# Weight tiles displaced inside their slots, so that moving and next stationary tile keep one distance, in a four-mixer transformer kernel

## The chip, the cores and the metric

The kernel runs on one core of a Trainium2 chip. The metric is device time in microseconds (us) of one execution, the median over several runs. TensorE (PE) multiplies: a 128x128 stationary tile is loaded by an LDWEIGHTS instruction, then a moving tile of 256 columns is streamed through it by a MATMUL. VectorE (DVE), ScalarE (ACT) and GpSimd (POOL) do the elementwise work; SyncE (SP) issues the transfers.

## The reference

A sequence of 256 tokens with 1,024 channels goes through four mixers (gated linear attention, differential attention, short convolution, causal block attention with ALiBi), two SwiGLU feed-forward layers and two gated embeddings, all in float32. Nearly all of the arithmetic is `norm(h) @ W` with 1,024 to 5,632 columns of W:

```
for i in range(DEPTH):                       # DEPTH = 2
    hn = rms_norm(h, norm_mix[i])
    h = h + (gla_mixer if i == 0 else diff_attn_mixer)(hn, ...)
    h = h + swiglu(rms_norm(h, norm_ffn[i]), ffn_w_in[i], ffn_w_out[i])
    gate = jax.nn.sigmoid(rms_norm(h, ple_norm[i]) @ ple_w_gate[i])
    h = h + gate * (p[i] @ ple_w_proj[i])
h = h + short_conv_mixer(rms_norm_2(h, norm_g[0]), ...)
h = h + moba_mixer(rms_norm_2(h, norm_g[1]), ...)
```

## The kernel before, in words

The activations stay on the chip. The weights, 159 MB, pass once through it in pieces of 128x1024 float32 (512 KB): a transfer into a `raw` buffer (`load`, L149 to L154), a rounded copy `whi` by ScalarE (`high`, L160) and the remainder `wlo = raw - whi` by VectorE (`low`, L169). The activations of a stage are split the same way into `xh` and `xl` (L292, L296), or `ah`, `al` inside a feed-forward layer. A product is then three float32r matmuls, high by high, high by low and low by high, in `mm3`:

```
nc.tensor.matmul(ps, lh, rh, start=first, stop=False, **kw)      # L214
nc.tensor.matmul(ps, lh, rl, start=False, stop=False, **kw)      # L215
nc.tensor.matmul(ps, ll, rh, start=False, stop=last, **kw)       # L216
```

`gemm` (L218) takes a piece as four blocks of 128x256 and issues, for each, two halves of 128 columns with three matmuls each, so 24 matmuls a piece. In most products the weights are **stationary** and the activations move (in the profile `g<-xh,whi`, the moving tile named first). In some, `natural=True`, the activations are stationary and the weights move (`g<-whi,xh`): all of `diff_i`, the chunks 4 to 7 of `gla_i` and 0 to 11 of `moba_i`.

`ahead` (L173) keeps the splitting three to five pieces ahead of PE: 4 `raw`, 6 `whi` and 5 `wlo` buffers. The elementwise work of the stages is queued by due times in units of pieces (the table `DL`), and PE, DVE and ACT each run their instructions in the fixed order in which this gives them out.

**Where the tiles lie.** SBUF addresses here are bytes within a partition. In the program as built before, the slots of `raw`, `whi` and `wlo` are 4,096 bytes each and begin at multiples of 512. So each stationary or moving piece of a weight begins at 0 modulo 512 (pieces are 512 or 1,024 bytes). A slot of `xh` is 2,112 bytes and one of `xl` 2,240 (`new_x`, L117): slot n of the eight begins at 64n (`xh`) and 192n (`xl`) modulo 512. `ah` and `al` begin at 128, the pair `px` of the embedding at 0.

Call D the start of the moving tile of one matmul less the start of the stationary tile that is loaded next, modulo 512. Before, D in the order of the three matmuls of `mm3` is, by slot:

| slot of the activations | weights stationary | weights moving |
|---|---|---|
| 0 | 0, 0, 0 | 0, 0, 0 |
| 1 | 64, 192, 64 | 448, 320, 448 |
| 2 | 128, 384, 128 | 384, 128, 384 |
| 3 | 192, 64, 192 | 320, 448, 320 |
| 4 | 256, 256, 256 | 256, 256, 256 |
| 5 | 320, 448, 320 | 192, 64, 192 |
| 6 | 384, 128, 384 | 128, 384, 128 |
| 7 | 448, 320, 448 | 64, 192, 64 |

A norm's four tiles lie in slots 0, 7, 6, 5, the next norm's in 4, 1, 2, 3 or an order of these; each slot serves 12 matmuls of a chunk of 48. For `ah` and `al` D is 128 throughout.

Of the kernel before, what the change touches and what calls it, by code (L numbers as in the profile page):

```python
# [13 lines left out]
F32R = mybir.dt.float32r  # L14
# [5 lines left out]
P = 128  # L20
D = 1024
KT = D // P
T = 256
# [3 lines left out]
CW = 2048  # L27
EXP_LN = "natural_log_exp_and_others"
AHEAD = 3
LINE = 128  # L30
FILL = 5
RAWS = 4
LAMBDA_INIT = 0.8 - 0.6 * math.exp(-0.3)

# [18 lines left out]
for _name, _n in (("ident", 128), ("dmask", 64)):  # L53
# [29 lines left out]
}  # L83

POOL = {"dkn", "dro", "gd", "ge", "go.0", "go.1", "gq", "gr", "ha.0", "ha.3", "ha.6", "mo2", "pa0", "pa1.0",
        "sqa"}

# [2 lines left out]
def body(ctx: ExitStack, tc: tile.TileContext, a, out: bass.AP):  # L90
    nc = tc.nc
# [4 lines left out]
    whip = ctx.enter_context(tc.tile_pool(name="whip", bufs=AHEAD + 3))  # L96
    wlop = ctx.enter_context(tc.tile_pool(name="wlop", bufs=AHEAD + 2))
    hp = ctx.enter_context(tc.tile_pool(name="hp", bufs=8))
    xp = ctx.enter_context(tc.tile_pool(name="xp", bufs=8))
# [15 lines left out]
        return hp.tile([P, 2, T], F32, tag="h", name="h")  # L115

    def new_x():  # L117


        return [xp.tile([P, 2 * T + rest], F32R, tag=n, name=n)[:, :2 * T].rearrange("p (j c) -> p j c", c=T)  # L120
                for n, rest in (("xh", 16), ("xl", 48))]

    def bank():
        return psg.tile([P, 2, T], F32, tag="g", name="g")
# [4 lines left out]
    def on(name, i=None):  # L129

        return nc.gpsimd if (f"{name}.{i}" in POOL or name in POOL) else nc.vector

# [11 lines left out]
    seq, now, side, seen = [], [0], [], []  # L144
# [3 lines left out]
    def load(limit=RAWS):  # L148
        while state["load"] < min(len(seq), state["lo"] + limit):  # L149
# [3 lines left out]
            raws[state["load"]] = raw  # L153
            state["load"] += 1  # L154

    def high():
        u = state["hi"]
        key, j, k0, kn, c = seq[u]
        hi = whip.tile([P, CW // 2], F32R, tag="whi", name="whi")
        nc.scalar.copy(hi[:, :kn * c], raws[u][:, :kn * c])  # L160
        his[u] = hi
        state["hi"] += 1

    def low():
        u = state["lo"]
        key, j, k0, kn, c = seq[u]
        hi = his.pop(u)
        lo = wlop.tile([P, CW // 2], F32R, tag="wlo", name="wlo")
        nc.vector.tensor_sub(lo[:, :kn * c], raws.pop(u)[:, :kn * c], hi[:, :kn * c].bitcast(F32))  # L169
        ready[u] = [(hi[:, k * c:(k + 1) * c], lo[:, k * c:(k + 1) * c]) for k in range(kn)]  # L170
        state["lo"] += 1

    def ahead():  # L173
        while True:
            load()
            if state["hi"] < min(len(seq), now[0] + AHEAD + 2):
                high()
            if state["lo"] >= min(len(seq), now[0] + AHEAD + 1):
                break
            low()  # L180
        load()
# [98 lines left out]
    class Norm:  # L280
# [6 lines left out]
        def part(self, i, h):  # L287
            p = self.gi
            xh, xl = new_x()
            gain = [sm("gain", p * 8 + 2 * i + j, 1) for j in range(2)]  # L290
            for j in range(2):
# [171 lines left out]
    def ffn_plan(layer):  # L463
# [4 lines left out]
        def done(ps, f):  # L468
            g, sg, t3 = t1(), t1(), t1()
            nc.vector.tensor_mul(g, ps[:, 0], N.rb)  # L470
            if f < 8:
                if f % 2 == 0:
                    S.spare = new_x()
                ah, al = S.spare[0][:, f % 2], S.spare[1][:, f % 2]
            else:
                ah, al = [S.fp.tile([P, T], F32R, tag=n, name=n, bufs=FT - 8) for n in ("ah", "al")]

            def lo():
                nc.vector.tensor_sub(al, t3, ah.bitcast(F32))
                S.act[f] = (ah, al)  # L480

            chain(layer, ("fs", lambda: nc.scalar.activation(sg, g, AF.Silu)),  # L482
                  ("fm", lambda: nc.vector.tensor_mul(t3, sg, ps[:, 1])),
                  ("fh", lambda: nc.scalar.copy(ah, t3)),
                  ("fl", lo))
# [13 lines left out]
    def gla_plan():  # L499
# [204 lines left out]
        def r_done(ps, h):  # L704
            b = SimpleNamespace()
            if h % 2 == 0:
                S.r4 = S.gp.tile([P, 2, 2, T], F32, tag="qk", name="rr", bufs=2)
            rr = S.r4[:, h % 2]
            nc.vector.tensor_mul(rr, ps, bc2(N.rb))

            def mul():
                b.o2 = t2()
                on("gr", h).tensor_mul(b.o2, S.on[h], rr)

            def hi():
                b.h, b.l = new_x()
                nc.scalar.copy(b.h, b.o2)

            def lo():
                nc.vector.tensor_sub(b.l, b.o2, b.h.bitcast(F32))  # L720
                S.og.update((2 * h + j, (b.h[:, j], b.l[:, j])) for j in range(2))

            chain(h, ("grs", lambda: nc.scalar.activation(rr, rr, AF.Silu)), ("grm", mul), ("grh", hi), ("grl", lo))
# [528 lines left out]
    nc.scalar.preload_act_table_set(EXP_LN)  # L1252
    fill = tiny.tile([P, 8 * FILL], F32, name="fill", bufs=1)
    nc.gpsimd.memset(fill, 0.0)
# [4 lines left out]
    for i in range(4):  # L1259
        h = new_h()  # L1260
        nc.sync.dma_start(h, a["xT"][:, 2 * i:2 * i + 2, :])
        if i % 2 == 0:
            load(1)
        give(0, i, h)
        until(1)
        if i % 2 == 0:
            high()
            low()
    for i in range(4):
        load(1)  # L1270
        if i < 3:
            high()
            low()
        until(i + 2)
        state["t"] = 0.0
# [135 lines left out]
```

## Time and profile before

| | |
|---|---|
| median of 3 runs | 961.05 us (960.43 to 961.59) |
| the profiled execution, its own time | 961.72 us |
| its span, first to last instruction | 959.9 us |
| mean granted TensorE clock | 0.993 |
| PE busy | 935.1 us (97%), 7,772 matmuls |
| DVE busy | 664.0 us (69%) |
| ACT busy | 556.8 us (58%) |
| HBM read | 158.81 MB, 167 GB/s over the span |

A matmul is recorded with some 280 ns, but the next one starts long before it ends. What a matmul costs in a dense stretch is therefore read from the distance between starts: the time between two rows of the timeline, or the length of a stretch over the number of matmuls in it. In the profile's names the buffer numbers are left out; the slots above are those of the built program, met in its fixed order.

### The profile page before, as it was taken

The page shows a single profiled execution, that of the slowest core. Times are in us where ns is not written, and L with a number is a line of the kernel's source. Part 1 is how long each engine was busy: PE and PEld are TensorE (multiplying, and loading weights), DVE is VectorE, ACT ScalarE, POOL GpSimd, SP SyncE. Part 2 cuts the span into 40 slices and gives each one's busy share as a digit, 9 for nine tenths or more (in the row PEclk, how much of TensorE's full clock was granted, in tenths as well). Part 3 has the DMA queues.
Part 4 walks back from the last instruction along what each step waited for, and adds up shares of the span by engine and source line. Part 5 has one row for each costly group of instructions (what it writes and reads, how often), then busy time and mean ns, then how long its engine had stood idle before and what let it go on. Part 6 is the DMA issues. An engine that isn't in the chain of part 4 may idle for free.

```text
span 959.9 us, 19012 instructions
## 1 busy us (share of the span) xinstructions
PE 935.1 (97%) x7772; PEld 922.8 (96%) x7772; DVE 664.0 (69%) x988; ACT 556.8 (58%) x951; POOL 118.8 (12%) x86
## 2 busy tenths in 40 slices
PE   7989999999999989999999999999999999999998
PEld 7989999999999989899999999999999999999998
DVE  5883777666655698998586666565886668776663
ACT  6955666544544565677674455444774435677762
POOL 1050320000001362210010000012210002000010
PEclk9999999999999999999999999999999999999999
DMA  8543366555555644343565555555556536543332
GB/s 262 172 133 120 126 204 220 187 186 186 177 182 179 220 132 150 111 143 100 173 212 198 184 189 181 171 191 186 165 185 201 188 121 220 182 133 123 120 111 88
DMA packets 48007, 161.09 MB, mean 168 GB/s; under 512 B 5456, under 2 KB 6096, under 8 KB 47920
## 3 DMA queue, kind: packets, MB, share of 16 engines
q1 hardware_dynamic: 47376, 158.87, 50.6%
q8 instruction: 61, 1.00, 0.4%
q10 hardware_dynamic: 544, 1.02, 0.4%
q14 instruction: 26, 0.21, 0.1%
HBM read 158.81 MB, written 1.05 MB: 167 GB/s over the span
## 4 chain that ended last, share of the span: by engine, by line
PE 80%; DVE 10%; DMA 3%; ACT 3%; issue 1%; POOL 1%; SPq 0%; ACTq 0%; DVEq 0%; POOLq 0%
PE g L216 24%; PE g L214 24%; PE g L215 24%; DVE wlo L169 4%; DMA raw<-in_gla_i 1%; DVE xl L296 1%; ACT whi L160 1%; PE m L214 1%; DVE t L449 1%; PE m L806 1%; PE m L984 1%; PE m L1184 1%; DMA raw<-in_ple_g 1%; PE m L641 1%; DMA raw<-in_moba_i 1%
## 5 line engine op out<-in xcount | busy, mean ns | idle before, releaser
L214 PE MATMUL g<-xh,whi 128*128 128x256 f32 (+1 forms) x1672 | 474.1, 284 | 7.0 <-ACT whi L160 6.6
L216 PE MATMUL g<-xh,wlo 128*128 128x256 f32 (+1 forms) x1672 | 472.3, 282 | 0.0
L215 PE MATMUL g<-xl,whi 128*128 128x256 f32 (+1 forms) x1672 | 471.1, 282 | 0.1
L169 DVE TENSOR_TENSOR wlo<-raw,whi 128x1024 fp32r<-128x1024 f32 (+2 forms) x315 | 381.3, 1216 | 91.5 <-PE g L216 51.3
L160 ACT CAST whi<-raw 128x1024 fp32r<-128x1024 f32 (+2 forms) x315 | 312.1, 996 | 132.4 <-PE g L215 100.1
L214 PEld LDWEIGHTS g<-xh,whi 128*128 128x128 f32 (+1 forms) x1672 | 316.1, 189 | 7.9 <-ACT whi L160 6.6
L215 PEld LDWEIGHTS g<-xl,whi 128*128 128x128 f32 (+1 forms) x1672 | 316.7, 189 | 0.6 <-DVE xl L296 0.3
L216 PEld LDWEIGHTS g<-xh,wlo 128*128 128x128 f32 (+1 forms) x1672 | 316.2, 189 | 0.2 <-DVE wlo L169 0.2
L214 PE MATMUL g<-whi,xh 128*128 128x256 f32 x448 | 130.4, 291 | 2.7 <-ACT xh L292 2.7
L216 PE MATMUL g<-whi,xl 128*128 128x256 f32 x448 | 126.7, 283 | 1.8 <-DVE xl L296 1.8
L215 PE MATMUL g<-wlo,xh 128*128 128x256 f32 x448 | 126.6, 283 | 0.0
L214 PEld LDWEIGHTS g<-whi,xh 128*128 128x128 f32 x448 | 86.0, 192 | 4.1 <-ACT xh L292 2.9
L216 PEld LDWEIGHTS g<-whi,xl 128*128 128x128 f32 x448 | 85.6, 191 | 2.5 <-DVE xl L296 2.3
L215 PEld LDWEIGHTS g<-wlo,xh 128*128 128x128 f32 x448 | 86.0, 192 | 0.1
L482 ACT ACTIVATE t<-t 128x256 f32<-128x256 f32 x44 | 18.4, 418 | 94.5 <-DVE t L470 94.5
L215 PE MATMUL g<-al,whi 128*128 128x256 f32 x224 | 63.0, 281 | 0.0
L216 PE MATMUL g<-ah,wlo 128*128 128x256 f32 x224 | 63.0, 281 | 0.0
L214 PE MATMUL g<-ah,whi 128*128 128x256 f32 x224 | 63.0, 281 | 0.0
L470 DVE TENSOR_TENSOR t<-g,rb 128x256 f32<-128x256 f32 x44 | 18.7, 424 | 61.6 <-PE g L216 61.2
L370 POOL TENSOR_TENSOR h<-h,pj 128x512 f32<-128x512 f32 x8 | 12.4, 1560 | 291.5 <-DVE h L386 285.2
L292 ACT ACTIVATE xh<-h,small 128x256 fp32r<-128x256 f32 x64 | 29.4, 502 | 31.0 <-DVE h L379 8.2
L312 POOL TENSOR_TENSOR acc<-acc,sq 128x512 f32<-128x512 f32 x16 | 27.9, 1742 | 149.7 <-ACT sq L305 149.7
(220 smaller groups left out, 1009.0 us busy)
## 6 DMA issues: line engine op xcount, KB each, us to landing
raw<-in_ffn_i SPq DMA_DIRECT2D x88, 512.0 KB, 3.9
raw<-in_ffn_o SPq DMA_DIRECT2D x40, 512.0 KB, 4.2
raw<-in_conv_i SPq DMA_DIRECT2D x32, 512.0 KB, 4.6
raw<-in_moba_i SPq DMA_DIRECT2D x32, 512.0 KB, 3.9
raw<-in_diff_i SPq DMA_DIRECT2D x24, 512.0 KB, 3.8
raw<-in_gla_i SPq DMA_DIRECT2D x23, 512.0 KB, 5.0
raw<-in_ple_g SPq DMA_DIRECT2D x16, 512.0 KB, 4.5
raw<-in_gla_o SPq DMA_DIRECT2D x5, 512.0 KB, 3.6
```

The source lines that it names most:

```text
L160: nc.scalar.copy(hi[:, :kn * c], raws[u][:, :kn * c])
L169: nc.vector.tensor_sub(lo[:, :kn * c], raws.pop(u)[:, :kn * c], hi[:, :kn * c].bitcast(F32))
L214: nc.tensor.matmul(ps, lh, rh, start=first, stop=False, **kw)
L215: nc.tensor.matmul(ps, lh, rl, start=False, stop=False, **kw)
L216: nc.tensor.matmul(ps, ll, rh, start=False, stop=last, **kw)
L292: nc.scalar.activation(xh[:, j], h[:, j], AF.Copy, scale=gain[j])
L296: nc.vector.scalar_tensor_tensor(xl[:, j], h[:, j], gain[j], xh[:, j].bitcast(F32), op0=ALU.mult, op1=ALU.subtract)
L312: on("sqa", p).tensor_add(self.acc, self.acc, q)
L370: nc.gpsimd.tensor_add(n, h, proj[p // 3][i])
L449: on(f"pm{i // 3}", layer).tensor_mul(m[:, j], t[:, j], proj[layer][i][:, j])
L470: nc.vector.tensor_mul(g, ps[:, 0], N.rb)
L482: chain(layer, ("fs", lambda: nc.scalar.activation(sg, g, AF.Silu)), ("fm", lambda: nc.vector.tensor_mul(t3, sg, ps[:, 1])), ("fh", lambda ...
```

## The change

The slots of `whi` and `wlo` grow from 4,096 to 4,608 bytes, and the tile is placed inside its slot: 192 bytes behind its begin where the weights move, 320 where they are stationary. The slots of `xh` and `xl` become 2,048 bytes each without padding, and so begin at 0 modulo 512. A filler tile (`fill`, cleared once at the start by POOL) grows from 160 to 544 bytes, by which `ah` and `al` also begin at 0. With weights stationary the moving tile begins at 0 and the next stationary at 320; with weights moving at 192 and at 0: D is 192 in both. The scratch reserved for descriptors of transfers goes from 16 KB to 8 KB; the last tile ends at byte 224,480 instead of 228,704.

No instruction is added, taken away or moved: on every engine the order is the same as before, apart from the line numbers and the width of the one memset (128x136 for 128x40).

```
-FILL = 5
+FILL = 17
...
+DIST = 192
+SLOT = 512
...
     def new_x():
-
-
-        return [xp.tile([P, 2 * T + rest], F32R, tag=n, name=n)[:, :2 * T].rearrange("p (j c) -> p j c", c=T)
-                for n, rest in (("xh", 16), ("xl", 48))]
+        return [xp.tile([P, 2, T], F32R, tag=n, name=n) for n in ("xh", "xl")]
...
+    def shifted(pool, name, u):
+        key, j = seq[u][:2]
+        moving = key == "diff_i" or key == "gla_i" and 4 <= j < 8 or key == "moba_i" and j < 12
+        o = (DIST if moving else SLOT - DIST) // 4
+        return pool.tile([P, CW // 2 + SLOT // 4], F32R, tag=name, name=name)[:, o:o + CW // 2]
+
     def high():
...
-        hi = whip.tile([P, CW // 2], F32R, tag="whi", name="whi")
+        hi = shifted(whip, "whi", u)
...
     def low():
...
-        lo = wlop.tile([P, CW // 2], F32R, tag="wlo", name="wlo")
+        lo = shifted(wlop, "wlo", u)
...
-    nc = bacc.Bacc("TRN2", target_bir_lowering=False, num_devices=1)
+    nc = bacc.Bacc("TRN2", target_bir_lowering=False, num_devices=1, dynamic_dma_scratch_size=8192)
```

## Rows read from the trace of the kernel before

**Rows 1.** The page's busy times: us, share of the span, instructions.
```profile
PE 935.1 (97%) x7772; PEld 922.8 (96%) x7772; DVE 664.0 (69%) x988; ACT 556.8 (58%) x951; POOL 118.8 (12%) x86
```
**Rows 2.** The chain of work that ended last, shares by engine.
```profile
PE 80%; DVE 10%; DMA 3%; ACT 3%; issue 1%; POOL 1%; SPq 0%; ACTq 0%; DVEq 0%; POOLq 0%
```
**Rows 3.** Waits: engine and line, for whom, us in total, times, longest.
```profile
ACT whi L160 <- PE g L215: 100.1, 92, 3.4
...
PE g L214 <- ACT whi L160: 6.6, 1, 6.6
```
**Rows 4.** Groups of matmuls by line and form: count, busy us, mean ns.
```profile
L214 PE MATMUL g<-xh,whi 128*128 128x256 f32 x1664 | 470.6, 283 | 0.4 <-ACT xh L292 0.4
...
L215 PE MATMUL g<-wlo,xh 128*128 128x256 f32 x448 | 126.6, 283 | 0.0
L215 PE MATMUL g<-al,whi 128*128 128x256 f32 x224 | 63.0, 281 | 0.0
```
**Rows 5.** Stretches: us, busy of PE, PEld, DVE, ACT, POOL; clock, DMA share, GB/s.
```profile
72.00:326.00 254.00, 254.00 (x2127) 253.42 (x2126) 157.77 (x210) 135.87 (x198) 22.64 (x14) 1.00 0.54 178
...
358.00:457.00 99.00, 94.78 (x784) 91.48 (x785) 89.92 (x183) 65.33 (x154) 17.27 (x13) 0.97 0.38 125
457.00:680.00 223.00, 223.00 (x1884) 222.90 (x1883) 142.14 (x188) 117.16 (x166) 15.50 (x10) 1.00 0.57 186
...
701.00:797.00 96.00, 95.48 (x801) 94.98 (x800) 67.11 (x115) 48.60 (x68) 0.00 (x0) 1.00 0.54 176
```
**Rows 6.** Timeline of PE, weights stationary, slots 0, 7, 6, 5 in turn.
```profile
165.24 0.28 PE L214 MATMUL g<-xh,whi 128*128 128x256 f32 x1
...
166.66 0.29 PE L214 MATMUL g<-xh,whi 128*128 128x256 f32 x1
...
168.08 0.28 PE L214 MATMUL g<-xh,whi 128*128 128x256 f32 x1
...
169.52 0.28 PE L214 MATMUL g<-xh,whi 128*128 128x256 f32 x1
...
170.93 0.28 PE L214 MATMUL g<-xh,whi 128*128 128x256 f32 x1
```
**Rows 7.** Timeline of PE, weights stationary, D 128 throughout: `ah` and `al`.
```profile
267.70 0.28 PE L214 MATMUL g<-ah,whi 128*128 128x256 f32 x1
...
277.66 0.28 PE L214 MATMUL g<-xh,whi 128*128 128x256 f32 x1
```
**Rows 8.** Timeline of PE, weights moving, slots 0, 7, 6, 5 in turn.
```profile
823.00 0.28 PE L216 MATMUL g<-whi,xl 128*128 128x256 f32 x1
...
824.43 0.28 PE L216 MATMUL g<-whi,xl 128*128 128x256 f32 x1
...
825.80 0.28 PE L216 MATMUL g<-whi,xl 128*128 128x256 f32 x1
...
827.21 0.28 PE L216 MATMUL g<-whi,xl 128*128 128x256 f32 x1
...
827.56 0.28 PE L216 MATMUL g<-whi,xl 128*128 128x256 f32 x1
...
828.58 0.28 PE L216 MATMUL g<-whi,xl 128*128 128x256 f32 x1
```
**Rows 9.** Timeline of PE, weights moving, slot 3.
```profile
371.01 0.28 PE L216 MATMUL g<-whi,xl 128*128 128x256 f32 x1
...
372.44 0.28 PE L216 MATMUL g<-whi,xl 128*128 128x256 f32 x1
```
**Rows 10.** Timeline of PE, weights stationary, slot 3.
```profile
510.18 0.28 PE L214 MATMUL g<-xh,whi 128*128 128x256 f32 x1
...
511.60 0.28 PE L214 MATMUL g<-xh,whi 128*128 128x256 f32 x1
```
**Rows 11.** L296, writing `xl` in all eight slots: ns min/median/max, first and last start.
```profile
L296 DVE SCALAR_TENSOR_TENSOR xl<-h,small,xh x64: 468/483/1522, 5.3 to 815.9; 128x256 fp32r<-128x256 f32 x64
```
**Rows 12.** DMA queues of the page: packets, MB, share of 16 engines.
```profile
q1 hardware_dynamic: 47376, 158.87, 50.6%
...
q10 hardware_dynamic: 544, 1.02, 0.4%
```

## The prediction

> **What bounds the kernel now.** I read the page's busy times first: PE is busy 97% of the span, DVE 69%, ACT 58% [rows 1]. A busy PE need not be a PE at its peak, so next come the chain and the waits. PE carries 80% of the chain that ended last [rows 2]. Its longest wait for anybody is 6.6 us, for the first weights; ACT, which makes those weights, waited 100.1 us for PE to give buffers back [rows 3]. So the splitting runs ahead and PE sets the pace. The stretches show where: from 72 to 326, 457 to 680 and 701 to 797 us PE is dense while DVE has 62%, 64% and 70% [rows 5]. Between 358 and 457 DVE has 91% and PE has gaps [rows 5]; there a faster PE is worth little.
>
> What does one matmul cost in a dense stretch? 223.00 us over 1,884 matmuls is 118.4 ns from start to start [rows 5]. The granted clock there is 1.00, that is 2.4 GHz, and 256 periods of that are 106.7 ns. A matmul of 256 columns takes 12 ns more than that here.
>
> How much more depends on where the tiles lie. With weights moving, four slots follow each other, 12 matmuls each, with the same shapes and the same piece structure [rows 8]. Slot 0 takes 1.43 us, 119.2 ns a matmul. Slot 7 takes 1.37 us (114.2), slot 6 takes 1.41 (117.5), slot 5 takes 1.37 (114.2). Within slot 5 the last nine take 1.02 us, **113.3 ns**: after three at the beginning the pattern settles and stays. With weights stationary [rows 6] slots 0 and 7 give 1.42 us (118.3), slot 6 gives 1.44 (120.0), slot 5 gives 1.41 (117.5); `ah` and `al`, at a constant D of 128, take 9.96 us for 84 (118.6) [rows 7]. Shapes and lines are the same in each comparison; what differs is the slot.
>
> **The change part by part.** What it alters on PE is D, made 192 everywhere, and which of the two tiles is off the multiple of 512.
>
> *Weights stationary.* L214, L215 and L216 with `xh` and `xl` are 3 x 1,664 matmuls, with `ah` and `al` 3 x 224 [rows 4]. After the change the moving tile begins at 0, the next stationary at 320. No row of before shows this pair throughout, but slot 5 with weights moving has it in two of three matmuls (stationary `xh` at 320, moving weights at 0), and the third has 448 and 0. That slot is the one that settles at 113.3 [rows 8]. This is the nearest row, and I take it. The bounds from the other rows: at best 113.3 from the first matmul on, at worst the 120.0 of slot 6 [rows 6]. I add 0.3 ns for the settling, which happens again after each interruption, and take 113.6.
>
> How many of them set the end? The dense stretches at 72 to 326, 457 to 680 and 701 to 797 hold 2,127 + 1,884 + 801 = 4,812 matmuls [rows 5]. About 120 of those are the mixer's own, by my estimate; 680 to 701 and the last mixer's end add about 550 more, half of them behind waits. I count 5,000. The cost now is 118.5 on average, between rows 5, 6 and 7. The saving is 5,000 x (118.5 - 113.6) = 24.5 us.
>
> The Trainium skill bears on how low this can go: TensorE: Matmul & The Clock Gate, section Back-to-back issue gap, gives N/2.4 + 2.5 ns for one isolated matmul, 109.2 ns at N = 256. By that figure the saving would be 5,000 x 9.3 = 46 us and the time about 915. No dense row here comes below 113.3, so the rows decide and this is no bound of mine.
>
> *Weights moving.* 3 x 448 matmuls [rows 4], moving tile at 192, next stationary at 0. The nearest row is slot 3 with weights stationary, which has this pair in two of three: 1.42 us for 12, 118.3 ns [rows 10]. Now the slots 0, 7, 6, 5 give 5.58 us for 48, 116.3 on average [rows 8]. So these may become 2 ns slower. About a third stand between 358 and 457 us, where DVE hides it; on the path I count 500: +1.0 us. The bounds are 113.3 (500 x 3 = 1.5 us gained) and 120.0 (1.9 us lost).
>
> *The writers.* ACT and DVE write `whi` and `wlo` at 192 or 320 instead of 0. The nearest row is L296, which writes `xl` at all eight residues: 64 of them with a minimum of 468 and a median of 483 ns [rows 11], so residues can't differ by much. Cost nothing; and were it 10 ns on 315 pieces, 3 us on DVE, the splitting's lead of 100.1 us of waiting [rows 3] covers it. If that cover went, the 3 us would be PE's.
>
> *Keeping PE fed.* At 113.6 ns a piece of 24 matmuls takes 2.73 us instead of 2.84. DVE's share from 457 to 680 goes from 64% to 66% [rows 5], the transfers from 186 to 194 GB/s. Neither is near its end. What is late next is the elementwise work at the stage borders; I give 1 us back for it.
>
> *The scratch and the filler.* All transfers of the weights and the others are in queues of the kind hardware_dynamic [rows 12], and no row shows a use of that scratch: nothing. The wider memset is one instruction on POOL at the start, on an engine busy 12% [rows 1]: nothing.
>
> The **sum** is -24.5 + 1.0 + 1.0 = -22.5 us against the profiled execution's own 961.72 us, so 939.2. That execution stands 0.67 us above the median of the runs, 961.05, so the forecast for the median is 938.5 us.
>
> **The rivals.**
>
> *A pattern in between.* With slot 3 the distances with weights stationary are 192, 64, 192, almost those of slot 5 with weights moving (192, 64, 192), yet the one takes 118.3 [rows 10] and the other 113.3 [rows 8]. So D alone does not decide; the place of the tiles does too. And weights moving at slot 3, with odd multiples of 64 as well, takes 1.43 us (119.2) [rows 9]. If 0 and 320 throughout give a repeating pattern like slot 5 of rows 6 (117.5) or a little better, say 117, the saving is 5,000 x 1.5 = 7.5 us: about 953.5. For it speaks that a constant D of 128 settles at no floor but at 118.6 [rows 7]; against it, that the very pair reached 113.3.
>
> *Slower.* A constant distance can also lock in a bad state: without the change of slots nothing throws the sequence out of it. The price is slot 6's 120.0 [rows 6]: 5,000 x 1.5 = 7.5 us more, about 969. It decides from a settled pitch above 118.5 ns. For it speaks that slot 0, with D constant at 0, takes 119.2 with weights moving [rows 8], among the worst; against it, that slot 5 goes from a slow beginning to 113.3 within three matmuls and does not leave it.
>
> *No change.* The pitch could belong to something that goes with the slot in time, not to the address, or PE's gain could be eaten by the splitting. Then 961, within the 0.2% (2 us) that a measurement of this kernel tells from no change. Rows 8 speak against the first, rows 3 and 5 against the second. The Trainium skill would have this outcome: SBUF — State Buffer, section Who interferes with whom, gives PE two independent read ports, one for the moving tile and one for LDWEIGHTS, and says that PE never waits on anyone. The trace disagrees so far: the same shapes take 119.2 and 113.3 ns by slot.
>
> That the change doesn't do what it says is excluded as far as addresses go: they follow from the slot sizes, and D comes out as 192 for both kinds.
>
> **How the numbers follow.** The forecast (the settled 113.3 with weights stationary) has 0.64, the pattern in between 0.17, no change 0.07, slower 0.12. Faster by over 0.2% is the first two, 0.81. The forecast's own range: at the low end 5,500 matmuls with weights stationary gain 5.2 ns each (28.6 us) and those with weights moving 1.5 us, nothing is lost at borders, about 931; at the high end the settling costs 1 ns, 4,700 count (19.7 us), and 2 us more are lost at borders, about 945. To hold 8 in 10 the range must reach the pattern in between: 931 to 954.
>
> **What would show it.** In the timeline of PE with weights stationary, starts 113 to 114 ns apart for the whole of a feed-forward layer, slots making no difference; the stretch that now takes 457 to 680 us shorter by 9 to 10 us; with weights moving 117 to 119 ns. DVE and ACT with the same mean durations. The forecast is wrong if weights stationary settle above 115 ns, or if PE settles at 113.3 and new waits on `whi` or `wlo` appear in the waits of PE.

## The result, and the profile after

The changed kernel takes **938.48 us** (median of 4 runs, 934.91 to 940.74) against 960.74 us (median of 4, 960.38 to 961.59) for the kernel before: a ratio of 0.9764, 95% interval 0.9729 to 0.9798. It is faster by 22.3 us; 938.5 was forecast. The profiled execution took 937.19 us by its own time, with a span of 935.3 us and a mean granted clock of 0.996.

The page's busy times of the changed kernel [before: rows 1], and the shares of its chain of waits by engine [rows 2]:

```profile
PE 909.9 (97%) x7772; PEld 896.7 (96%) x7772; DVE 660.6 (71%) x988; ACT 555.9 (59%) x951; POOL 120.6 (13%) x86
...
PE 82%; DVE 9%; ACT 2%; POOL 2%; DMA 2%; issue 1%; SPq 0%; POOLq 0%; ACTq 0%; DVEq 0%
```

PE is busy 25.2 us less with the same 7,772 matmuls, and the span is 24.6 us shorter; the three other engines are busy as before, within 4 us. The limit has not moved. Waits of the changed kernel (engine and line, for whom, total us, times, longest); the code's lines lie 8 further down than before [rows 3]:

```profile
ACT whi L168 <- PE g L223: 88.7, 87, 3.4
...
PE g L222 <- ACT whi L168: 6.3, 1, 6.3
```

The splitting still waits for PE, 88.7 us in place of 100.1, and PE's one long wait for weights is the one at the start. Beyond that one, no wait of PE for `whi` or `wlo` is longer than 0.3 us. Neither the writer of `xl` [rows 11] nor that of `wlo` pays for its new place (lines of the source: ns minimum/median/maximum, first and last start, forms); before, `wlo` had 556/1218/3131:

```profile
L304 DVE SCALAR_TENSOR_TENSOR xl<-h,small,xh x64: 472/484/1525, 5.5 to 792.4; 128x256 fp32r<-128x256 f32 x64
...
L177 DVE TENSOR_TENSOR wlo<-raw,whi x315: 557/1218/3134, 6.3 to 921.7; 128x1024 fp32r<-128x1024 f32 x140, 128x512 fp32r<-128x512 f32 x17, 128x384 fp32r<-128x384 f32 x1
```

So the whole gain is in how PE runs. Two stretches of the changed kernel, with the columns of rows 5; the first is the counterpart of 457 to 680 there:

```profile
442.00:664.00 222.00, 222.00 (x1956) 221.90 (x1955) 146.09 (x195) 123.21 (x174) 16.58 (x11) 1.00 0.59 194
684.00:776.00 92.00, 92.00 (x783) 92.00 (x782) 63.67 (x109) 44.53 (x61) 0.00 (x0) 1.00 0.56 186
```

To turn a count into a pitch (the distance from start to start): a stretch also counts the two or three matmuls that began up to 0.28 us before it, so the pitch is the stretch plus 0.28 us, divided by the count. The first stretch gives 222.28 / 1,956 = 113.6 ns; in the second it is 92.28 / 783 = 117.9. The place and the distance of the tiles are the same in both, and so is the granted clock, 1.00 (2.4 GHz).

PE alone, by stretches (us, busy, matmuls, clock, DMA share, GB/s). Before:

```profile
200.00:300.00 100.00, 100.00 (x846) 1.00 0.56 183
690.00:750.00 60.00, 59.48 (x497) 1.00 0.56 185
```

After; the first three have weights stationary, the last has them moving:

```profile
200.00:300.00 100.00, 100.00 (x885) 1.00 0.58 190
480.00:580.00 100.00, 100.00 (x885) 1.00 0.62 205
690.00:750.00 60.00, 60.00 (x512) 1.00 0.59 198
41.00:55.00 14.00, 14.00 (x121) 1.00 0.43 145
```

Before, the feed-forward layer at 200 to 300 us runs at 100.28 / 846 = 118.5 ns. After, both layers run at 113.3, the short convolution (690 to 750) at 117.7, and weights moving at 41 to 55 us at 118.0. There are **two settled patterns**, 113.3 and 117.8 ns, and a stretch keeps the one it has. The timeline shows where it changes, some 60 matmuls into the convolution's stage (start, duration, engine, line, tiles; in brackets idle time and what ended it):

```profile
676.28 0.28 PE L222 MATMUL g<-xh,whi 128*128 128x256 f32 x1
...
677.19 0.28 PE L224 MATMUL g<-xh,wlo 128*128 128x256 f32 x1
678.76 0.38 PE L222 MATMUL g<-xh,whi 128*128 128x256 f32 x1 [1.29 <-ACT xh L300]
...
680.67 0.70 PE L337 MATMUL m<-ssum,ones 128*128 128x256 f32 x2
...
681.67 0.28 PE L223 MATMUL g<-xl,whi 128*128 128x256 f32 x1
...
683.91 0.28 PE L224 MATMUL g<-xh,wlo 128*128 128x256 f32 x1
```

Up to 677.19 eight distances make 0.91 us (113.8, with starts rounded to 10 ns). Then PE waits 1.29 us for the last tile of the stage's norm, and is interrupted once more by that norm's own sums (`m<-ssum,ones`). From 681.67 on, 19 distances make 2.24 us, 117.9 ns. Nothing interrupts PE for the next 886 matmuls, and all of them stay at 117.8. In the kernel before PE waits for the same tile, but for 0.39 us only:

```profile
701.63 0.38 PE L214 MATMUL g<-xh,whi 128*128 128x256 f32 x1 [0.39 <-ACT xh L292]
```

So the whole stage of the convolution gains next to nothing. Its first matmul (960 matmuls ahead of the next stage) and the first of that next stage, where the weights move again, in the kernel before and then in the changed one:

```profile
693.95 0.28 PE L214 MATMUL g<-xh,whi 128*128 128x256 f32 x1
...
809.32 0.28 PE L214 MATMUL g<-whi,xh 128*128 128x256 f32 x1
```

```profile
670.50 0.28 PE L222 MATMUL g<-xh,whi 128*128 128x256 f32 x1
...
785.79 0.28 PE L222 MATMUL g<-whi,xh 128*128 128x256 f32 x1
```

115.37 us before, 115.29 after. Read in the same way, each feed-forward layer gains 8.0 to 8.2 us (188.0 and 188.2 to 180.0), the first mixer with what leads up to it 4.5, the two embeddings 0.9 and 1.0, the second mixer, which DVE holds back, 0.8, and the last mixer with the end 1.1. With the convolution's 0.1 this is the 24.6 us of the span.

### The profile page after: what moved, and what is told of

The parts are those of the page before. It is cut to its first block, busy times and chain, and to the rows that moved or that the text cites. A ratio compares the mean times of both kernels' runs of the same rounds, so it can differ in the third digit from the quotient of the medians.

```text
span 935.3 us, 19012 instructions
## 1 busy us (share of the span) xinstructions
PE 909.9 (97%) x7772; PEld 896.7 (96%) x7772; DVE 660.6 (71%) x988; ACT 555.9 (59%) x951; POOL 120.6 (13%) x86
## 4 chain that ended last, share of the span: by engine, by line
PE 82%; DVE 9%; ACT 2%; POOL 2%; DMA 2%; issue 1%; SPq 0%; POOLq 0%; ACTq 0%; DVEq 0%
PE g L222 25%; PE g L223 25%; PE g L224 25%; DVE wlo L177 3%; PE m L222 1%; DVE xl L304 1%; ACT whi L168 1%; PE m L814 1%; PE m L992 1%; DMA raw<-in_gla_i 1%; POOL h L462 1%; PE m L1192 1%; DVE t L457 1%; DMA h<-in_xT 1%; PE m L223 1%
## 5 line engine op out<-in xcount | busy, mean ns | idle before, releaser
L222 PE MATMUL g<-xh,whi 128*128 128x256 f32 (+1 forms) x1672 | 468.6, 280 | 7.6 <-ACT whi L168 6.3
L224 PE MATMUL g<-xh,wlo 128*128 128x256 f32 (+1 forms) x1672 | 465.4, 278 | 0.3 <-DVE wlo L177 0.3
L223 PE MATMUL g<-xl,whi 128*128 128x256 f32 (+1 forms) x1672 | 465.2, 278 | 0.1
L168 ACT CAST whi<-raw 128x1024 fp32r<-128x1024 f32 (+2 forms) x315 | 311.6, 995 | 121.6 <-PE g L223 88.7
L304 DVE SCALAR_TENSOR_TENSOR xl<-h,small,xh 128x256 fp32r<-128x256 f32 x64 | 37.0, 618 | 14.7 <-ACT xh L300 14.7
```

The costliest lines, as they stand in the source:

```text
L304: nc.vector.scalar_tensor_tensor(xl[:, j], h[:, j], gain[j], xh[:, j].bitcast(F32), op0=ALU.mult, op1=ALU.subtract)
```

## The experiments

At first the question was what the gain hangs on. The prediction said the distance D and the place of the tiles together (theory A in what was expected); the others were that D alone decides (B), that any constant D does, since the slots no longer alternate (C), and that D = 192 has two patterns and something else draws between them (D). In what follows "pitch" is worked out from windows as above. Where stretches are counted, they are runs of more than 20 matmuls with no distance of 140 ns or more, and the pitch of one is that of its last twelve distances. In the changed kernel 17 of these with weights stationary end at 113.3 and 13 at 117.8; with weights moving 26 and 16.

**e1_zero: D constant at 0.**

```
-DIST = 192
+DIST = 0
```

> The change with a distance of 0 instead of 192: every moving and every stationary tile begins at a multiple of 512, everything else is as in the changed kernel. Theory A (the pair of places decides: stationary at 320 with moving at 0 settles at 113.3 ns): starts 120.0 ns apart almost everywhere, time about 966 to 970 us, slower than before. Theory B (the distance alone decides): the same. Theory C (any constant distance does, since nothing then throws the sequence out of its pattern): 113 to 115 ns, 935 to 943 us.

970.57 us, beside 958.35 for the kernel before on that chip.

```profile
200.00:300.00 100.00, 100.00 (x836) 1.00 0.56 180
```

100.28 / 836 = 120.0 ns, and all 71 counted stretches settle there. A constant distance alone is no gain; the wrong one costs 12 us.

**e2_place: D stays 192, the tiles lie elsewhere.** A pad of 192 bytes ahead of the activations puts these at 192; stationary weights lie at 0, moving ones at 384.

```
+    pad = xp.tile([P, DIST // 4], F32, tag="pad", name="pad", bufs=1)
+    tc.nc.gpsimd.memset(pad, 0.0)
...
-        o = (DIST if moving else SLOT - DIST) // 4
+        o = (2 * DIST if moving else 0) // 4
```

> The same distance of 192 everywhere, but other places: all tiles of activations begin at 192, stationary weights at 0, moving weights at 384. Theory A: with weights stationary the pair (moving 192, next stationary 0) is that of slot 3 before, 117 to 118.5 ns, 953 to 961 us. Theory B: as in the changed kernel, stretches at 113.3 and stretches at 117.8 ns, 934 to 942 us. Theory C: as B.

954.01 us, a time in the range of the theory that the place decides. The trace doesn't bear it out:

```profile
200.00:300.00 100.00, 100.00 (x851) 1.00 0.57 184
469.00:487.00 18.00, 18.00 (x161) 1.00 0.77 243
```

The first feed-forward layer has 100.28 / 851 = 117.8 ns, but 469 to 487 us, the same kind of matmul in the same tiles, has 18.28 / 161 = 113.5. Both patterns are there at the new place too (12 stretches at 113.3 and 17 at 117.8 with weights stationary, 32 and 8 with weights moving); this time the long ones are at 117.8. So the place alone does not decide between 113.3 and 117.8. The time alone would have led to the wrong reading.

**e3_stationary_only: D = 192 only where weights are stationary.** Moving weights go back to 0, so D is 0 there.

```
-        o = (DIST if moving else SLOT - DIST) // 4
+        o = (0 if moving else SLOT - DIST) // 4
```

> Only the stationary weights are displaced (320); moving weights begin at 0 as the activations do, distance 0. What this part of the change is worth: theories A and B: with weights moving 119 to 120 ns instead of 115.6, of which only the dense stretches count, so 1 to 4 us slower than the changed kernel, 938 to 944 us; with weights stationary 113.3 or 117.8 ns as in the changed kernel. Theory C: no difference to the changed kernel, 935 to 941 us.

941.39 us. Stretches of PE with weights stationary and then moving:

```profile
200.00:300.00 100.00, 100.00 (x885) 1.00 0.58 188
...
41.00:55.00 14.00, 14.00 (x119) 1.00 0.41 137
```

113.3 ns as in the changed kernel, and 14.28 / 119 = 120.0 with weights moving (all 41 stretches). This loses 3 us by the times, or 5 to 6 by the ratios to the kernel before on the same chip. With weights moving it is slower than the kernel before (120.0 against 117.1 ns on average), and yet 17 us faster as a whole: most of the gain is in the stationary weights.

**e4_scan: one D after another in one run.** Each pair of chunks (four pieces, 96 matmuls) of the feed-forward layers' first product and of the convolution's gets its own D in steps of 16 bytes, the last two steps stand in the output products of the last two mixers, and all else keeps 192. Its time mixes all of them and isn't read.

```
+        if key == "ffn_i":
+            dist = 16 * (j // 2)
+        elif key == "conv_i":
+            dist = 16 * (22 + j // 2)
+        elif key in ("conv_o", "moba_o"):
+            dist = 480 if key == "conv_o" else 496
+        else:
+            dist = DIST
+        o = (dist if moving else SLOT - dist) // 4
```

> A scan of the distance with weights stationary: moving tiles stay at 0, the stationary ones of each pair of chunks of ffn_i, then conv_i, then conv_o and moba_o, are placed so that the distance grows from 0 to 496 in steps of 16, some 96 matmuls at each; all other products keep 192. Only the pitch at each distance is read, not the time. Theory A and B: 113.3 ns around 192 and at 64, near 120 at 0 and 256, 118 to 119 at 128 and 384, and a curve between. Theory C: 113 to 115 ns at every distance after a few matmuls. Nobody of these says what multiples of 16 between the multiples of 64 do.

The timeline at the borders of blocks of 96 matmuls; between two rows lies one D, first 16 to 128, then 288 to 320:

```profile
145.69 0.28 PE L232 MATMUL g<-xh,wlo 128*128 128x256 f32 x1
...
157.20 0.28 PE L232 MATMUL g<-xh,wlo 128*128 128x256 f32 x1
...
168.41 0.28 PE L232 MATMUL g<-xh,wlo 128*128 128x256 f32 x1
...
179.61 0.28 PE L232 MATMUL g<-xh,wlo 128*128 128x256 f32 x1
...
190.91 0.28 PE L232 MATMUL g<-xh,wlo 128*128 128x256 f32 x1
...
202.25 0.28 PE L232 MATMUL g<-xh,wlo 128*128 128x256 f32 x1
...
213.75 0.28 PE L232 MATMUL g<-xh,wlo 128*128 128x256 f32 x1
...
225.26 0.28 PE L232 MATMUL g<-xh,wlo 128*128 128x256 f32 x1
...
236.65 0.28 PE L232 MATMUL g<-xh,wlo 128*128 128x256 f32 x1
...
557.09 0.28 PE L232 MATMUL g<-xh,wlo 128*128 128x256 f32 x1
...
568.30 0.28 PE L232 MATMUL g<-xh,wlo 128*128 128x256 f32 x1
...
579.50 0.28 PE L232 MATMUL g<-xh,wlo 128*128 128x256 f32 x1
...
590.80 0.28 PE L232 MATMUL g<-xh,wlo 128*128 128x256 f32 x1
```

Differences over 96 give 119.9 ns at D = 16, 116.8 at 32, 116.7 at 48, 117.7 at 64, 118.1 at 80, 119.8 at 96, 119.9 at 112 and 118.6 at 128; then 116.8 at 288, 116.7 at 304 and 117.7 at 320. D and D + 256 give the same, in all sixteen pairs of the scan to 0.2 ns: the effect has a period of 256 bytes, not of 512 as the change takes it.

In the scan no step reached 113.3, not even 192, which is one of them (489 to 500 us here). But 192 comes twice more in this run, in the second product of each layer and what follows it:

```profile
262.00:326.00 64.00, 64.00 (x568) 1.00 0.63 198
489.00:499.90 10.90, 10.90 (x95) 1.00 0.75 251
606.00:671.00 65.00, 65.00 (x554) 1.00 0.56 179
```

That is 64.28 / 568 = 113.2, 117.7 and 117.8 ns. PE was not interrupted at the change of D: from 143.1 to 327.6 us and from 486.1 to 672.8 no distance between starts reaches 140 ns. What differs is the D that ran just before, 160, 176 and 336; in the changed kernel, with 192 throughout, both layers run at 113.3. So what preceded can set the pattern without any wait, and the scan shows, for each D, the pattern in which it was entered and not that there is no other.

**e8_again: the changed kernel once more**, unaltered, to see whether the slow stretches stay where they were.

> The changed kernel once more, unaltered. Theory D (one distance of 192 allows two settled patterns, 113.3 and 117.8 ns, and what the sequence finds after each interruption depends on when it starts): the same two pitches, but in part in other stretches than in the first profile, and a time somewhere between 933 and 944 us. Theory E (the stretch decides, by its weights, its load or its transfers: 680 to 797 us is slow by itself): again 113.3 ns up to 680 us and 117.8 from there to 797 us.

937.50 us.

```profile
480.00:580.00 100.00, 100.00 (x885) 1.00 0.63 207
690.00:750.00 60.00, 60.00 (x512) 1.00 0.61 202
```

With weights stationary the same stretches are fast and slow, 113.3 and 117.7 here (17 and 13, as before); with weights moving some differ. That speaks for something slow in those stretches themselves, which the next two runs test.

**e5_alt64 and e6_alt192: an alternation with weights stationary.** `whi` and `wlo` get different places, so D goes 64, 192, 64 or 192, 64, 192 over the three matmuls of `mm3`; weights moving stay as in the change. For e5:

```
-        o = (DIST if moving else SLOT - DIST) // 4
+        o = (DIST if moving else 448 if name == "whi" else 320) // 4
```

For e6:

```
-        o = (DIST if moving else SLOT - DIST) // 4
+        o = (DIST if moving else 320 if name == "whi" else 448) // 4
```

> With weights stationary, whi at 448 and wlo at 320, moving tiles at 0: the distances of the three matmuls are 64, 192, 64 instead of a constant 192, as in slot 7 of the kernel before with weights moving, which reached 113.3 ns after one matmul. Weights moving as in the changed kernel. Theory F (an alternation with moving tiles that stay in place leaves only the 113.3 pattern): 113.3 to 113.6 ns in all dense stretches, 929 to 934 us. Theory D with nothing special in the alternation: both pitches again, 933 to 944 us.

> The same with whi at 320 and wlo at 448: distances 192, 64, 192, as in slot 5 of the kernel before with weights moving. Theory F: 113.3 to 113.8 ns in all dense stretches, 929 to 935 us. Theory D with nothing special in the alternation: both pitches, 933 to 944 us.

e5 takes 945.29 us, outside what either theory gave.

```profile
200.00:300.00 100.00, 100.00 (x885) 1.00 0.58 189
480.00:580.00 100.00, 100.00 (x844) 1.00 0.60 196
690.00:750.00 60.00, 59.72 (x521) 1.00 0.61 203
```

113.3 ns in the first layer, 100.28 / 844 = 118.8 in the second: 64, 192, 64 has two patterns as well (12 and 18 stretches), and the second of them is 1.0 ns worse than the changed kernel's 117.8. The fast and slow stretches lie elsewhere than in the changed kernel, so the stretches themselves are not the cause.

e6 takes **934.55 us**. All 29 counted stretches with weights stationary end at 113.3, those of the convolution among them. That the one order leaves a single pattern and the other two was not foretold by any theory, and stays unexplained.

**e7_scratch_only: the kernel before with 8 KB of scratch.**

```
-    nc = bacc.Bacc("TRN2", target_bir_lowering=False, num_devices=1)
+    nc = bacc.Bacc("TRN2", target_bir_lowering=False, num_devices=1, dynamic_dma_scratch_size=8192)
```

> The kernel before with the smaller scratch alone: all tiles lie 8,192 bytes lower, so every place modulo 512 and every distance stays. If the places modulo 512 explain the change: the same time as before within 0.3%, and the same pitch by slot. If the scratch or the absolute address matters: nearer to the changed kernel.

960.83 us beside 960.17.

```profile
200.00:300.00 100.00, 100.00 (x846) 1.00 0.56 183
```

The same count of matmuls as in the kernel before. Neither the scratch nor the move of every tile by 8,192 bytes does anything that shows.

**e9_alt192_timed and e10_changed_timed**: the kernel of e6 and the changed kernel, unaltered, timed beside each other on one chip in five rounds.

> The kernel of e6 (whi at 320, wlo at 448 with weights stationary) once more, timed against the kernel before in five rounds. Theory F (this alternation leaves only the pattern of 113.3 ns): 932 to 936 us, and runs closer together than those of the changed kernel (934.9 to 940.7). Theory D (e6 was lucky in what it found after each interruption): a spread like the changed kernel's, median 936 to 940 us, stretches at 117.8 or 118.9 ns in its profile.

> The changed kernel beside e9 on the same chip, five rounds. Theory D: median 936 to 940 us with a spread of 3 us or more, 2 to 5 us above e9. If the two do not differ by more than 1 us, the stretches at 117.8 ns of the changed kernel cost nothing that e9 wins back.

e9 takes 935.0 us (median of 4, 932.68 to 936.31), 0.9733 of the time before (0.9716 to 0.975). The changed kernel takes 938.57 (median of 5, 935.69 to 941.53), 0.9775 (0.9753 to 0.9797); the kernel before 960.16 (median of 9). The intervals don't overlap: e9 beats both kernels, the changed one by 3.6 us. Its runs spread over 3.6 us, those of the changed kernel over 5.8 and those of the kernel before over 2.9. PE alone in e9:

```profile
480.00:580.00 100.00, 100.00 (x884) 1.00 0.62 206
690.00:750.00 60.00, 60.00 (x532) 1.00 0.65 212
```

From 690 to 750 us there are 532 matmuls where the changed kernel has 512: 113.3 ns instead of 117.7. The convolution's stage, read as above, takes 111.3 us (673.54 to 784.87) instead of 115.3. These 4.0 us are all of the 3.9 by which the spans of the two profiled executions differ (932.7 and 936.6); what the other stages lose and gain cancels.

**e11_alt_moving: e6, and an alternation with weights moving too**, where now the moving tile is the one that jumps.

```
-        o = (DIST if moving else SLOT - DIST) // 4
+        hi = name == "whi"
+        o = ((192 if hi else 64) if moving else 320 if hi else 448) // 4
```

> e6, and with weights moving whi at 192 and wlo at 64: distances 192, 64, 192 there too, but now the moving tile jumps while the stationary one stays at 0. If the distances decide alone: 113.3 to 114.5 ns with weights moving, instead of 115.6, and 1 to 2 us less than e6, 932 to 934 us. If it matters which of the two jumps (slot 3 of the kernel before had this with weights stationary and took 118.3): 117.5 to 118.5 ns, and 1 to 3 us more, 935 to 938 us.

936.25 us. Weights stationary stay at 113.3 (all 30). With weights moving, 24 distances in e11:

```profile
799.46 0.28 PE L223 MATMUL g<-whi,xh 128*128 128x256 f32 x1
...
802.28 0.28 PE L223 MATMUL g<-whi,xh 128*128 128x256 f32 x1
```

and 24 in the changed kernel in about the same place of the program:

```profile
798.13 0.28 PE L222 MATMUL g<-whi,xh 128*128 128x256 f32 x1
...
800.85 0.28 PE L222 MATMUL g<-whi,xh 128*128 128x256 f32 x1
```

2.82 / 24 = 117.5 against 2.72 / 24 = 113.3 ns. In e11 all 42 stretches with weights moving end at 117.8; none reaches 113.3. The distances are 192, 64, 192 as in e6. What differs is **which tile jumps**: there the stationary one, here the moving one. That the weights are stationary in the one product and move in the other is not the reason, as far as twelve matmuls show it: before, slot 5 with weights moving has the stationary tile jump and settles at 113.3 [rows 8], slot 3 with weights stationary has the moving tile jump and takes 118.3 [rows 10].

**e12_48: D constant at 48**, the best of the scan's steps.

```
-DIST = 192
+DIST = 48
```

> A constant distance of 48 for both kinds of product. In the scan this distance had 116.7 ns from its second matmul on. If the scan foretells a whole kernel: 116.7 ns everywhere with weights stationary, no stretch at 113.3 and none above 117, 948 to 952 us. If there are several patterns here too: stretches at other pitches.

954.02 us, above what was expected.

```profile
200.00:300.00 100.00, 100.00 (x860) 1.00 0.57 186
```

100.28 / 860 = 116.6 ns with weights stationary, as the scan gave, in all 29 stretches; with weights moving, of which the expectation gave no pitch, it is 118.3 in all 40. So at 48 it matters which of the two tiles is the weight, or where they lie. That was not taken further.

## Why the prediction was right, and where not

The forecast for the median held to 0.1 us, which is closer than its terms deserve, and in part luck: two terms were off and nearly made up for each other, and the runs of the changed kernel spread over 5.8 us. The profiled execution, for which the terms were added up, took 937.19 us where the sum gave 939.2.

*What bounds the kernel* was read rightly. PE set the pace before and after [rows 2, 3], and the stretches that gained most gained by their pitch. DVE's share of 66% and the 194 GB/s of the transfers came as forecast (442 to 664 us).

*Weights stationary, 113.6 ns.* This term is the step that failed. "The pattern settles and stays" holds, but not for one pattern: the mean over all distances below 140 ns is 114.4 ns, since 13 of 30 stretches, the convolution's long one among them, settle at 117.8. By the prediction's own sign of being wrong, a settled pitch above 115 ns, it failed in these. By the prediction's own count that is 5,000 x (118.5 - 114.4) = 20.5 us in place of 24.5. The count was too low as well: with some 5,660 matmuls [rows 4] it is 23.2. Rate and count together were off by 1.3 us only.

*The nearest row.* The prediction took slot 5 with weights moving [rows 8] for the change's own pair. e6 and e11 show what it really was. In that slot the stationary tile jumps between 320 and 448 and the moving one lies at 0: that is e6, which knows only 113.3. Slot 3 with weights stationary [rows 10] has the same three distances with the moving tile jumping: that is e11 in kind, at 118.3 and 117.8. So "D alone does not decide" was right; "the place does too" was not shown, since a constant 192 has both pitches at either place (e2), though at 48 something besides D does matter (e12). The variable missing for these two rows is which tile carries the alternation. A constant 192 is neither of them, and has both pitches.

*Weights moving.* They were to become 2 ns slower and cost 1.0 us. They became faster, 117.1 to 115.6 ns on average, as 26 of 42 stretches reach 113.3. On the 500 matmuls counted on the path that is a gain of 0.7 us. The nearest row there, slot 3 with weights stationary, was an alternating pair again, not a constant one.

*Writers, scratch, filler*: nothing, as said (the medians above, and e7). *Borders*: the 1 us given back was about right. The wait at the convolution's border grew from 0.39 to 1.29 us, by 0.9. Together 23.2 + 0.7 - 0.9 = 23.0 of the 24.6 us in the span are accounted for. If all 1,344 matmuls with weights moving counted, and not 500, it would be 24.3; how many do is not shown.

*The rivals.* The pattern in between did come, in part of the stages: it is the 117.8. "Slower" was a real hazard, though not at 192: e1 shows the constant bad pattern, at 120.0 ns and 970.6 us. That is 12 us over the kernel before on its chip, where 7.5 were given to it, as its products with weights moving are slower too. "No change" fell. The Trainium skill, SBUF — State Buffer, section Who interferes with whom, would have it so, with PE's two read ports independent and PE never waiting; the runs disagree, since kernels that differ in tile addresses alone go from 934.6 us (e6) to 970.6 (e1, on another chip, 1.8 us quicker with the kernel before), at 113.3 to 120.0 ns a matmul. Where in the reading of the tiles this arises, in the ports or behind them, no run shows.

*The spread.* The changed kernel's runs spread over 5.8 us, both times, those of before over 1.2 and 2.9. Stretches that fall to one pattern or the other by run would do that, but the record does not show it: in the three profiled executions of the changed kernel (937.19, 937.50, 938.51 us) all stretches with weights stationary from 34 us on have the same pattern each time, and the feed-forward layers, the embeddings and the convolution take the same time to 0.1 us. What differs there is the time of the first two mixers and the last, by 0.9 to 1.4 us each.

What stays open: how what preceded, an interruption or another distance, sets the pattern; why 192, 64, 192 leaves one pattern and 64, 192, 64 two; why D = 48 differs between the kinds; whether other constant distances have a second pattern that the scan did not enter. An alternation for weights moving in which the stationary tile jumps throughout was not tried.

## What to carry to other kernels

When matmuls follow each other without a wait, read their pitch from the distance of starts, stretch by stretch: the same instructions can settle at two pitches 4% apart and stay there until the next interruption, and a mean hides it. Where the pitch differs by buffer, try the offsets of moving and stationary tiles against each other; here places inside slots that grew by 512 bytes were worth 22 to 25 us of 960. And test the offsets that the good buffer really had, not the tidier version of them: the alternation 192, 64, 192 in the stationary tile gave 935.0 us, the constant 192 gave 938.6.

## What the runs showed of the hardware that was not expected

- The pitch of one and the same float32r matmul with its weight load goes from 113.3 to 120.0 ns with the relative place of the moving tile and the next stationary one, at a granted clock of 1.00. No settled stretch came below 113.3. The Trainium skill, TensorE: Matmul & The Clock Gate, section Back-to-back issue gap, has 109.2 ns for an isolated matmul of 256 columns; no settled stretch here, where each matmul has its own weight load, reached it.
- The effect repeats every 256 bytes (e4: 116.8 ns at 32 and at 288, 117.7 at 64 and at 320, and so in all sixteen pairs).
- One distance can have two stable pitches (192: 113.3 and 117.8; 64, 192, 64: 113.3 and about 118.8). An interruption of PE, as by the two matmuls of a norm's sums at 680.67 us, can end in the other one, and 886 matmuls in a row then stay in it. So can a change of distance without any interruption (e4: 192 runs at 113.2 ns behind 160 and at 117.7 behind 176).
- The two tiles are not alike: 192, 64, 192 settles at 113.3 when the stationary tile alternates (e6, 29 of 29) and at 117.8 when the moving one does (e11, 42 of 42).
